# Squared norms and state reads as column-quarter products in a hybrid decoder step

## The chip, the cores and the metric

The kernel runs on one core of a Trainium2 chip. The time is device microseconds (us) of one execution. TensorE (PE) multiplies, VectorE (DVE), ScalarE (ACT) and GpSimd (POOL) do the element-wise work, SyncE (SP) issues most transfers. Each engine works through a queue of its own in the order fixed when the kernel is built; semaphores join the queues.

## The reference, cut to what matters

One inference step of a decoder layer for a prompt of 512 tokens and eight sample sequences with one token each. A projection feeds sparse attention (NSA) and a gated DeltaNet side by side; then come a merge, an output projection and an MLP. The change touches two places of the DeltaNet half.

```python
q, k, v = split(silu(conv(qkv)))          # 8 heads of 128 channels
q = _l2norm(q); k = _l2norm(k)            # x * rsqrt(sum(x*x over 128 channels) + EPS)
...
def step(state, xs):                      # for the sample: one token, state 128 x 128 per head and sequence
    v_new = u_c - w_c @ state             # reads the state by k
    o = q_c @ state + a_c @ v_new         # reads the state by q
    state = state * exp(gl_c) + k_c.T @ v_new
```

## The kernel before, in words

Channels lie on the 128 partitions, tokens along the free dimension: 512 of the prompt, then 8 of the samples. The fp32 inputs of the large products are split into two rounded parts, and `step` (L413) multiplies them in three products per slice of 128 channels (`bpg`, L153). These projections are cut into units of 128 output channels; they form one long stream. Everything else (recurrence, attention, the sample's work) is written as Python generators that `run` (L471) interleaves with the stream by an account of TensorE time, `pe_time`; each `yield n` asks for so much of the stream in between. A scheduler then orders the instructions of each engine at build time, by priority and by its own estimate of when operands are ready; so the order on an engine is not the order in the source.

**Quarters.** `quarters` (L163) makes four products that each write 32 partitions of one PSUM bank, partitions 32j to 32j+31, with a weight 32 columns wide. I call four of them with different j a *four*. They use different column quarters of the array. The first may be placed anywhere; the other three are only kept in order behind it, so other products may stand between them. Callers are the modulation projection (`ada`, L253: weight matrix `wa`, two fours in a row for each of 24 units), the sample's attention scores (`skT,Qz`, L1659, 8 fours) and its values (`arena` with `consts`, `pg` or `kvN`, L1697, 14 fours). All of these move 256 columns in fp32.

**Squared norms.** `norms` (L576) is called for each of 8 k heads (`ev_k`, L584) and 8 q heads (`ev_q`, L609), as soon as the projection of the head is evacuated, convolved and squared (tile `pre`). Four products with a column of ones, one for each 128 tokens, put the sum of the squares of a token into one PSUM column with tokens on partitions; DVE adds EPS, POOL raises it to -1/2, DVE makes two derived factors (`brk`, `brk2` or `rq`, `rq2`).

**State reads.** `dn_sample` (L1247) loads the sample's state in pieces of 128 x 4 x 128 (`Sx`, two for each of 8 heads). `read` (L1330) multiplies each of the 8 states of a head, as the weight, with the two columns `kq` (k and q of this sequence); six small DVE operations make `vn` of it. `vn` is turned (`consts,vn`), an outer product (`vbd,kst`) updates `Sx`, and SP writes it back (L1370) and loads the head after next (L1317).

**Buffers.** PSUM tags `ek` and `pg` have two banks each, `sp` (also called `sc`, `pt`) four. The SBUF tag `s2k` has four slots for `Sx`, pages and rows; `acc` (L1787), the sum of squares for the second norm, is a fifth user of it. `e2k` has four slots for evacuated rows.

fp32 products that are not transposes run as two instructions each in the trace; transposes and rounded products as one.

Of the kernel before, what the change touches and what calls it, by code (L numbers as in the profile page):

```python
# [7 lines left out]
F32 = mybir.dt.float32  # L8
# [3 lines left out]
ALU = mybir.AluOpType  # L12
# [5 lines left out]
T = S + NB  # L18
# [4 lines left out]
EPS = 1e-6  # L23
# [2 lines left out]
C_Q, C_KV, C_NG, C_DN, C_Z, C_A, C_B, C_M = 0, 1024, 2560, 2608, 5680, 6704, 6712, 6720  # L26
NRAW = 4
NKEEP = 8
CW = 3664
CR = 1024  # L30
SLOT = 528
ON_Q = "vector"
# [37 lines left out]
def hybrid_step(ctx: ExitStack, tc: tile.TileContext, A, O, dbg=None):  # L70


    nc = tc.nc
# [5 lines left out]
    wk = ctx.enter_context(tc.tile_pool(name="wk", bufs=10))  # L79
# [27 lines left out]
    def e2(name, dt=F32):  # L107
        return wk.tile([128, SLOT], dt, name=name, tag="e2k", bufs=4)
# [8 lines left out]
    def cst(shape, dt):  # L117

        n = 1
        for v in shape[1:]:  # L120
            n *= v
        r = dt == F32R
        x = (rounded if r else consts)[0:shape[0], cused[r]:cused[r] + n]
        cused[r] += -(-n // 8) * 8
        assert cused[r] <= (CW, CR)[r]
        x = x.bitcast(dt) if dt == I32 else x
        return x if len(shape) == 2 else x.rearrange("p (a b) -> p a b", a=shape[1])
# [12 lines left out]
    def bank(tag):  # L140
        tag = "sp" if tag in ("sc", "pt") else tag
        return ps.tile([128, 512], F32, name="b" + tag, tag=tag, bufs=4 if tag == "sp" else 2)
# [9 lines left out]
    def mm(out, lhs, rhs, start, stop):  # L152
        nc.tensor.matmul(out, lhs, rhs, start=start, stop=stop)  # L153
        n = 1
        for v in rhs.shape[1:]:
            n *= v
        pe_time[0] += n * (1 if rhs.dtype == F32R else 4) / 2400.0

    def tr(out, in_, idn):
        nc.tensor.transpose(out, in_, idn)  # L160
        pe_time[0] += 0.107

    def quarters(out, lhs, rhs, start, stop, n=1, order=(3, 2, 1, 0)):  # L163

        first = True
        for s in range(n):
            for j in order:
                r = nc.tensor.matmul(out[32 * j:32 * j + 32], lhs(j, s), rhs(j, s), start=start and s == 0, stop=stop and s == n - 1)
                if not first:
                    tc.keep_in_program_order(r)  # L170
                first = False
        pe_time[0] += 0.25 * n * rhs(0, 0).shape[-1] / 128
# [5 lines left out]
    for hf in range(2):  # L178
        c = slice(hf * 512, hf * 512 + 512)
# [11 lines left out]
    for t in range(5):  # L191
        src, n = x_rows(t)
# [18 lines left out]
    ident = cst([128, 128], F32)  # L211
    nc.vector.tensor_scalar(ident, jp, 0.0, None, op0=ALU.is_equal)
    ones = cst([128, 128], F32)
    nc.vector.memset(ones, 1.0)
    mhalf = cst([128, 8], F32)
    nc.vector.memset(mhalf, -0.5)
    cT = cst([128, 96], F32)
    nc.vector.memset(cT, 0.0)
    sel = cst([128, 9], F32)
    nc.vector.tensor_tensor(sel, ident[:, 0:9], ident[:, 32:41], op=ALU.add)  # L220
    for j in (64, 96):
# [334 lines left out]
    rq, rq2, brk = (smp[:, 96 + i * 32:128 + i * 32].rearrange("p (h c) -> p h c", c=4) for i in range(3))  # L556
    nsb, lns, brk2 = (smp[:, 192 + i * 32:224 + i * 32].rearrange("p (c h) -> p c h", h=DH) for i in range(3))
    slot = {}
# [14 lines left out]
        return out, e  # L573


    def norms(out, sq, eps):  # L576

        p = bank("ek")
        for t in range(4):
            mm(p[:, t:t + 1], sq[:, t * 128:(t + 1) * 128], ones[:, 0:1], start=True, stop=True)  # L580
        nc.vector.tensor_scalar(out, p[:, 0:4], eps, None, op0=ALU.add)
        nc.gpsimd.tensor_tensor(out, out, mhalf[:, 0:4], op=ALU.pow)

    def ev_k(i, P):  # L584
        y, e = yield from conv(8 + i, P, slot["kT"][:, i])
        nc.scalar.activation(e, slot["kT"][:, i], AF.Square)
        yield
        yield
        r = lns[:, :, i]
        norms(r, e, EPS)  # L590
        nc.vector.tensor_tensor(brk[:, i], r, slot["beta"][:, :, i], op=ALU.mult)
        nc.vector.tensor_tensor(brk2[:, :, i], r, brk[:, i], op=ALU.mult)

    tma, o_dn = Whole(), Whole()

    def bv(h, c):
        return o_dn[:, h, c * 128:(c + 1) * 128]
# [11 lines left out]
    def ev_q(i, P):  # L609
        y, e = yield from conv(i, P, slot["qT"][:, i])  # L610
        nc.scalar.activation(e, y, AF.Square)
        yield
        yield
        r = rq2[:, i]
        norms(r, e, EPS)
        nc.vector.tensor_scalar(rq[:, i], r, float(128 ** -0.5), None, op0=ALU.mult)
        nc.vector.tensor_tensor(r, rq[:, i], rq[:, i], op=ALU.mult)

    V = []

# [108 lines left out]
    for x in FILL.split():  # L729
        if x in nxt:  # L730
            n = nxt[x]
# [19 lines left out]
    for j in range(8):  # L751
        if j < 5:
            norm1(j)
        i = j // 2 + 4 * (j % 2)
# [447 lines left out]

    def nsa_tiles():

        masks = wk.tile([128, SLOT], F32, name="masks", tag="masks", bufs=1)
        mk = slot["mk"] = masks[:, 0:512]
        jp = token_gap()
        mc = slot["mc"] = cst([128, 4, 32], F32)
        with tc.issue_after(slot["late_v"].ins):
            nc.vector.memset(mk[:, 0:384], 0.0)  # L1210
            nc.vector.tensor_scalar(mk[:, 384:512], jp, 0.0, BM, op0=ALU.is_gt, op1=ALU.mult)
            for i in range(4):
                nc.vector.tensor_scalar(mc[:, i], cio, float(128 * i), BM, op0=ALU.is_gt, op1=ALU.mult)
        Kt = b16("K", F32R)
        Ks = slot["Ks"] = Kt[:, 0:2176].rearrange("p (g c) -> p g c", g=4)
        slot["Kw"] = Kt[:, 2176:4224].rearrange("p (g c) -> p g c", g=4)
        for g in range(NG):
            hi, lo = group_rows(g)
            with tc.issue_after(slot["late_a"].ins):
                nc.scalar.copy(out=Ks[hi, g, 0:32], in_=kcd[hi, g])  # L1220
            nc.vector.tensor_tensor(Ks[lo, g, 0:32], kcd[hi, g], f32(Ks[hi, g, 0:32]), op=ALU.subtract)
# [25 lines left out]
    def dn_sample():  # L1247
        dsc = kb4(q4, (1024,), F32, "dsc", "q4")
        r_k, r_q, qks, egs, bts, os_ = (dsc[:, i * 64:i * 64 + 64] for i in range(6))
        sy = dsc[:, 448:640].rearrange("p (m n) -> p m n", n=NB)  # L1250
        sq3 = dsc[:, 640:832].rearrange("p (a u) -> p a u", a=3)
        kq = dsc[:, 832:960].rearrange("p (u a) -> p u a", a=2)
# [15 lines left out]
        for hf in range(2):  # L1268
            p = bank("sc")
# [23 lines left out]
        p = bank("sc")  # L1293
# [18 lines left out]
        Sx = {}  # L1312
# [8 lines left out]
        for hf in range(2):  # L1321
            p = bank("sc")
# [7 lines left out]
        def read(h):  # L1330

            us = slice(h * 8, h * 8 + 8)
            p = bank("sc")
            for hf in range(2):
                for n in range(4):
                    u = h * 8 + hf * 4 + n
                    mm(p[:, (hf * 4 + n) * 2:(hf * 4 + n) * 2 + 2], Sx[h][hf][:, n], kq[:, u], start=True, stop=True)
            ks = p[:, 0:16].rearrange("p (n a) -> p a n", a=2)
            vn = wk.tile([128, 3, 8], F32, name="vn", tag="vn", bufs=4)
            nc.vector.tensor_tensor(vn[:, 0], ks[:, 0], egs[:, us], op=ALU.mult)  # L1340
            nc.vector.tensor_tensor(vn[:, 1], ks[:, 1], egs[:, us], op=ALU.mult)
            nc.vector.tensor_tensor(vn[:, 0], v_s[:, us], vn[:, 0], op=ALU.subtract)
            nc.vector.tensor_tensor(vn[:, 0], vn[:, 0], bts[:, us], op=ALU.mult)
            nc.vector.tensor_tensor(vn[:, 2], vn[:, 0], qks[:, us], op=ALU.mult)
            nc.vector.tensor_tensor(os_[:, us], vn[:, 1], vn[:, 2], op=ALU.add)
            return vn
        vn = read(0)
        for h in range(8):
            yield 4
            pv = bank("pt")  # L1350
            tr(pv[0:8, 0:128], vn[:, 0], ident)
            if h < 7:
                vn = read(h + 1)
            vr = vst[h % 2]
            vs = f32(vr)
            nc.scalar.copy(out=vr[0:8], in_=pv[0:8, 0:128])
            nc.vector.tensor_copy(vr[64:72], vs[0:8])
            nc.vector.tensor_tensor(vr[32:40], pv[0:8, 0:128], vs[0:8], op=ALU.subtract)
            r = [v4(e2("vbd", F32R)[0:72, 0:512]) for _ in range(2)]
            for hf in range(2):  # L1360
                nc.vector.tensor_tensor(r[hf], vs[:, None, :].to_broadcast([72, 4, 128]),
                                        m72[:, hf * 4:hf * 4 + 4, None].to_broadcast([72, 4, 128]), op=ALU.mult)
            yield 4
            for hf in range(2):
                p = bank("pt")
                mm(p, kst[h // 4][:, h % 4], r[hf].rearrange("p n v -> p (n v)"), start=True, stop=True)
                for n in range(4):
                    u = h * 8 + hf * 4 + n
                    nc.vector.scalar_tensor_tensor(Sx[h][hf][:, n], Sx[h][hf][:, n], egs[:, u:u + 1], v4(p)[:, n], op0=ALU.mult, op1=ALU.add)
                nc.sync.dma_start(sdo[:, hf * 4:hf * 4 + 4, h], Sx[h][hf])  # L1370
            if h < 6:
                s_load(h + 2)
# [411 lines left out]
                nc.vector.tensor_tensor(xi[:, S:T], xi[:, S:T], e, op=ALU.add)  # L1784
        return halves(P, f, hv)

    acc = wk.tile([128, SLOT], F32, name="acc", tag="s2k", bufs=4)[:, 0:T]  # L1787

    def ev_out(hf):
        c = half(hf)  # L1790

# [174 lines left out]
```

## Time and profile before

| | us |
|---|---|
| median of 3 runs | 1334.24 |
| lowest, highest | 1331.4, 1338.27 |
| profiled execution, its own time | 1336.41 |
| span of that execution | 1334.6 |

The profile comes from one execution. Its span is the time from the first to the last instruction; 1.8 us lie around it. In a row of products, the start times tell how long one holds TensorE: products are pipelined, so that each row's duration is longer than the distance to the next start. The granted TensorE clock was 0.962 of full speed on the mean.

| engine | busy us | share |
|---|---|---|
| PE | 1262.5 | 95% |
| DVE | 849.2 | 64% |
| ACT | 645.9 | 48% |
| POOL | 253.5 | 19% |

### The profile page before, as it was taken

The numbers are of one execution on the slowest core, as the hardware profiler recorded it, in microseconds if no ns is written. First come the engines' busy times: TensorE is split into PE (matmuls) and PEld (weight loads), VectorE is DVE, ScalarE is ACT, GpSimd is POOL, SyncE is SP. The second block draws the span as 40 slices with busy tenths as digits, with TensorE's granted clock in tenths as the row PEclk, the third lists the DMA queues.
The fourth block names the chain that finished last, engine by engine and source line by source line (L and its number), as shares of the span: only waits on it lengthen the run. The fifth ranks groups of instructions, "written<-read, shape, count | busy, mean of one in ns | idle before, by whom it ended". The sixth has DMA issues, their size and how long they took to land. (4 is left out here: it accounts for less than half of the span.)

```text
span 1334.6 us, 26655 instructions
## 1 busy us (share of the span) xinstructions
PE 1262.5 (95%) x10336; PEld 1189.2 (89%) x10336; DVE 849.2 (64%) x2328; ACT 645.9 (48%) x1540; POOL 253.5 (19%) x338
## 2 busy tenths in 40 slices
PE   4999899999899999899999899999999999999997
PEld 3799899999689999787778798889999999999997
DVE  2696958894345788876677777795853334334355
ACT  3484848653243335555555766684543142142233
POOL 2102100212111110312132233230242021021000
PEclk9799999998698999899999999999999999999999
DMA  8843311423333455335334211544642332424252
GB/s 250 255 135 107 101 49 49 117 83 94 119 111 92 116 142 156 106 97 155 93 114 140 82 55 33 143 129 110 163 112 75 97 94 81 110 80 117 74 158 96
DMA packets 235875, 149.82 MB, mean 112 GB/s; under 512 B 10331, under 2 KB 231059, under 8 KB 235485
## 3 DMA queue, kind: packets, MB, share of 16 engines
q1 hardware_dynamic: 226436, 135.84, 36.2%
q0 software_dynamic: 2240, 6.38, 1.6%
q10 hardware_dynamic: 7072, 5.90, 1.5%
q8 instruction: 81, 1.33, 0.4%
q14 instruction: 46, 0.37, 0.1%
HBM read 136.87 MB, written 15.60 MB: 114 GB/s over the span
## 5 line engine op out<-in xcount | busy, mean ns | idle before, releaser
L153 PE MATMUL bpg<-hh,wh 128*128 128x264 f32 (+1 forms) x1168 | 340.9, 292 | 6.8 <-ACT pre L493 1.4
L153 PE MATMUL bpg<-hh,wl 128*128 128x256 f32 (+1 forms) x1168 | 336.5, 289 | 2.1 <-DVE wl L398 2.1
L153 PE MATMUL bpg<-hl,wh 128*128 128x264 f32 (+1 forms) x1168 | 336.7, 288 | 0.0
L153 PEld LDWEIGHTS bpg<-hh,wh 128*128 128x128 f32 x1168 | 224.8, 193 | 9.6 <-issue 1.9
L398 DVE TENSOR_TENSOR wl<-raw,wh 128x1024 fp32r<-128x1024 f32 x149 | 182.7, 1228 | 69.7 <-ACT wh L394 51.6
L153 PEld LDWEIGHTS bpg<-hh,wl 128*128 128x128 f32 x1168 | 223.9, 192 | 3.6 <-DVE wl L398 3.0
L153 PEld LDWEIGHTS bpg<-hl,wh 128*128 128x128 f32 x1168 | 224.7, 192 | 1.6 <-issue 0.4
L394 ACT CAST wh<-raw 128x1024 fp32r<-128x1024 f32 x117 | 121.3, 1047 | 160.5 <-PE bpg L153 150.6
L153 PE MATMUL bpg<-act,wh 128*128 128x264 f32 (+1 forms) x1024 | 185.7, 283 | 0.0
L153 PEld LDWEIGHTS bpg<-act,wh 128*128 128x128 f32 x1024 | 157.4, 188 | 0.1
L153 PE MATMUL bpg<-act,wl 128*128 128x264 f32 (+1 forms) x512 | 144.7, 283 | 0.2 <-DVE wl L398 0.2
L153 PE MATMUL bpg<-h2h,wl 128*128 128x256 f32 (+1 forms) x448 | 126.8, 283 | 0.0
L153 PE MATMUL bpg<-h2h,wh 128*128 128x256 f32 (+1 forms) x448 | 126.5, 282 | 0.0
L153 PE MATMUL bpg<-h2l,wh 128*128 128x256 f32 (+1 forms) x448 | 126.2, 282 | 0.0
L1819 POOL TENSOR_TENSOR r<-r 128x520 f32<-128x520 f32 (+2 forms) x40 | 59.6, 1490 | 285.7 <-ACT r L1818 281.4
L1780 DVE SCALAR_TENSOR_TENSOR o_dn<-bpg,consts,o_dn 128x256 f32<-128x256 f32 x80 | 38.4, 483 | 98.3 <-PE bpg L153 98.2
L153 PEld LDWEIGHTS bpg<-act,wl 128*128 128x128 f32 x512 | 96.2, 188 | 0.5 <-DVE wl L398 0.4
L153 PEld LDWEIGHTS bpg<-h2l,wh 128*128 128x128 f32 x448 | 84.5, 189 | 0.0
L153 PEld LDWEIGHTS bpg<-h2h,wl 128*128 128x128 f32 x448 | 84.3, 188 | 0.0
L153 PEld LDWEIGHTS bpg<-h2h,wh 128*128 128x128 f32 x448 | 84.1, 188 | 0.0
L1446 POOL TENSOR_SCALAR consts<-consts,scl 128x32 f32<-128x32 f32 x64 | 25.7, 405 | 252.1 <-DVE scl L1441 87.6
L153 PE MATMUL bsp<-K,qst 128*128 128x288 f32 (+6 forms) x288 | 70.7, 320 | 2.2 <-DVE mx L1409 0.9
(625 smaller groups left out, 2571.1 us busy)
## 6 DMA issues: line engine op xcount, KB each, us to landing
raw<-in_w_in SPq DMA_DIRECT2D x68, 512.0 KB
wa<-in_w_ada SPq DMA_DIRECT2D x48, 512.0 KB
raw<-in_w_down SPq DMA_DIRECT2D x40, 512.0 KB
raw<-in_w_up SPq DMA_DIRECT2D x36, 512.0 KB
raw<-in_w_out SPq DMA_DIRECT2D x12, 512.0 KB
Sx<-in_state_dn SPq DMA_DIRECT2D x16, 256.0 KB
out_s_dn<-Sx SPq DMA_DIRECT2D x16, 256.0 KB
pg<-in_cache_k_slc SPq DMA_DIRECT2D x16, 128.0 KB
```

The costliest lines, as they stand in the source:

```text
L153: nc.tensor.matmul(out, lhs, rhs, start=start, stop=stop)
L394: nc.scalar.copy(out=wh, in_=raw)
L398: nc.vector.tensor_tensor(wl[:, 0:kp], raw[:, 0:kp], f32(wh[:, 0:kp]), op=ALU.subtract)
L1446: nc.gpsimd.tensor_scalar(x, x, sc[:, a_ * 3 + b_:a_ * 3 + b_ + 1], 1.0, op0=ALU.mult, op1=ALU.mult)
L1780: nc.vector.scalar_tensor_tensor(xi[:, q], p[:, 0:n], mod[:, m + i, 0:1], xi[:, q], op0=ALU.mult, op1=ALU.add)
L1819: nc.gpsimd.tensor_tensor(r, r, r, op=ALU.mult)
```

## The change

It does four things. (1) In `quarters`, the second to fourth product of each four (and all later rounds of the call) get a very high priority, so that the scheduler places them right behind the first. (2) `norms` now makes one four per head: the weight is a window of 32 columns of a constant that holds ones in one column only, the 512 squared tokens move past it as four times 128 columns, and the head's sums land in row h of each quarter. Four heads accumulate into one bank of `ek`, which they hold from the first head to the fourth. Then ACT copies the bank (`nrm`), one transpose turns it, and DVE and POOL work on 4 x 4 columns at once. (3) `read` takes the columns `kq` as the weight (32 of them, a pair of heads) and moves the state: two fours for a head, an ACT copy (`rd`), two transposes, then the same six DVE operations; there is a `yield 1.5` after the copy. (4) `acc` takes the tile of the attention masks in place of a slot of `s2k`. Constants grow by 72 columns.

```diff
@@ quarters
         for s in range(n):
             for j in order:
-                r = nc.tensor.matmul(out[32 * j:32 * j + 32], lhs(j, s), rhs(j, s), start=start and s == 0, stop=stop and s == n - 1)
+                with nullcontext() if first else tc.high_priority(20000):
+                    r = nc.tensor.matmul(out[32 * j:32 * j + 32], lhs(j, s), rhs(j, s), start=start and s == 0, stop=stop and s == n - 1)
@@ constants
+    one_of = cst([128, 64], F32)
+    nc.vector.memset(one_of, 0.0)
+    nc.vector.memset(one_of[:, 31:32], 1.0)
@@ norms
-    def norms(out, sq, eps):
-
+    norm_bank = {}
+
+    def norms(i, out, sq):
+
+        h = i % 4
+        if h == 0:
+            norm_bank[0] = bank("ek")
+        p = norm_bank[0]
+        quarters(p[:, 0:128], lambda j, s: one_of[:, 31 - h:63 - h], lambda j, s: sq[:, j * 128:j * 128 + 128], h == 0, h == 3)
+        if h < 3:
+            return
+        e = e2("nrm")[:, 0:128]
+        nc.scalar.copy(out=e, in_=p[:, 0:128])
+        yield
         p = bank("ek")
-        for t in range(4):
-            mm(p[:, t:t + 1], sq[:, t * 128:(t + 1) * 128], ones[:, 0:1], start=True, stop=True)
-        nc.vector.tensor_scalar(out, p[:, 0:4], eps, None, op0=ALU.add)
-        nc.gpsimd.tensor_tensor(out, out, mhalf[:, 0:4], op=ALU.pow)
+        tr(p[:, 0:128], e, ident)
+        t = wk.tile([128, 4, 4], F32, name="nsq", tag="nsq", bufs=2)
+        nc.vector.tensor_scalar(t, p[:, 0:128].rearrange("p (c h) -> p h c", c=4)[:, 0:4], EPS, None, op0=ALU.add)
+        nc.gpsimd.tensor_tensor(out, t, mhalf.rearrange("p (h c) -> p h c", h=4), op=ALU.pow)
@@ ev_k (ev_q likewise, with rq2 and rq)
-        r = lns[:, :, i]
-        norms(r, e, EPS)
-        nc.vector.tensor_tensor(brk[:, i], r, slot["beta"][:, :, i], op=ALU.mult)
-        nc.vector.tensor_tensor(brk2[:, :, i], r, brk[:, i], op=ALU.mult)
+        hs = slice(i - 3, i + 1)
+        r = lns[:, :, hs].rearrange("p c h -> p h c")
+        yield from norms(i, r, e)
+        if i % 4 == 3:
+            nc.vector.tensor_tensor(brk[:, hs], r, slot["beta"][:, :, hs].rearrange("p c h -> p h c"), op=ALU.mult)
+            nc.vector.tensor_tensor(brk2[:, :, hs].rearrange("p c h -> p h c"), r, brk[:, hs], op=ALU.mult)
@@ read
             p = bank("sc")
+            kq_ = kq[:, h // 2 * 16:h // 2 * 16 + 16].rearrange("p u a -> p (u a)")
             for hf in range(2):
-                for n in range(4):
-                    u = h * 8 + hf * 4 + n
-                    mm(p[:, (hf * 4 + n) * 2:(hf * 4 + n) * 2 + 2], Sx[h][hf][:, n], kq[:, u], start=True, stop=True)
-            ks = p[:, 0:16].rearrange("p (n a) -> p a n", a=2)
+                quarters(p[:, hf * 128:hf * 128 + 128], lambda j, s: kq_, lambda j, s: Sx[h][hf][:, j], True, True)
+            e = e2("rd")[:, 0:256]
+            nc.scalar.copy(out=e, in_=p[:, 0:256])
+            yield 1.5
+            p = bank("sc")
+            for hf in range(2):
+                tr(p[:, hf * 128:hf * 128 + 128], e[:, hf * 128:hf * 128 + 128], ident)
+            ks = [p[:, h % 2 * 16 + a:h % 2 * 16 + a + 239:34] for a in range(2)]
...
@@ nsa_tiles, and where acc stood
-        masks = wk.tile([128, SLOT], F32, name="masks", tag="masks", bufs=1)
+        masks = acc.t = wk.tile([128, SLOT], F32, name="masks", tag="masks", bufs=1)
...
-    acc = wk.tile([128, SLOT], F32, name="acc", tag="s2k", bufs=4)[:, 0:T]
```

What this makes of the order, at three places. On TensorE, in the sample's scores; `skT,Qz` are the quarters, `pg` transposes of cache pages, `bpg`, `K,qst` and `V` products of the stream and of the prompt's attention. Before:

```order
L153 MATMUL bpg<-hl,wh 128x256
L168 MATMUL bek<-skT,Qz 32x256
L153 MATMUL bek<-ptl,V_5904 128x256
L153 MATMUL bek<-pth,V_5904 128x256
L153 MATMUL bek<-ptl,V_5904 128x256
L160 MATMUL bsp<-consts,pg 128x128
L168 MATMUL bek<-skT,Qz 32x256
L160 MATMUL bsp<-consts,pg 128x128
L168 MATMUL bek<-skT,Qz 32x256
L160 MATMUL bsp<-consts,pg 128x128
L168 MATMUL bek<-skT,Qz 32x256
L160 MATMUL bsp<-consts,pg 128x128
```

The same four after:

```order
L153 MATMUL bpg<-hh,wl 128x264
L160 MATMUL bsp<-consts,ps 128x128 x2
L160 MATMUL bsp<-consts,pw 128x128
L169 MATMUL bek<-skT,Qz 32x256 x4
L160 MATMUL bsp<-consts,pw 128x128
L160 MATMUL bsp<-consts,pg 128x128 x8
```

One four stood in four separate places between other products, and now stands in one.

On TensorE at the norm of a q head, the fourth of its group after the change; `pre` is the tile of squares. Before:

```order
L153 MATMUL bpg<-hh,wh 128x264
L153 MATMUL bpg<-hl,wh 128x264
L153 MATMUL bpg<-hh,wl 128x264
L153 MATMUL bek<-consts,pre 128x1 x4
L153 MATMUL bpg<-hh,wh 128x264
```

After, with `nrm` the copy that ACT makes between the two steps:

```order
L153 MATMUL bpg<-hl,wh 128x264
L153 MATMUL bpg<-hh,wl 128x264
L169 MATMUL bek<-pre,consts 32x128 x4
L160 MATMUL bek<-consts,nrm 128x128
L153 MATMUL bpg<-hh,wh 128x256
```

Four products of one column became a four of 128 columns, and the transpose follows it with no product between.

On TensorE at the third state read; `consts,vn` turns the head before, `grhs` and `rt` are the recurrence. Before:

```order
L153 MATMUL bpg<-hh,wh 128x256
L153 MATMUL bsp<-grhs,rounded 128x512
L160 MATMUL bsp<-consts,vn 8x128
L153 MATMUL bsp<-dsc,Sx 128x2 x8
L153 MATMUL bsp<-grhs,rounded 128x512
```

After:

```order
L153 MATMUL bsp<-rt,LU 128x128 x4
L153 MATMUL bsp<-grhs,rounded 128x512
L160 MATMUL bsp<-consts,vn 8x128
L169 MATMUL bsp<-Sx,dsc 32x128 x8
L153 MATMUL bpg<-hh,wl 128x256
```

Eight products with two columns each became two fours; their two transposes (`consts,rd`) stand 26 rows further down.

## Rows read from the trace of the kernel before

**Rows 1.** Page, parts 1 and 2: busy time of engines; tenths and granted clock in 40 slices.
```profile
PE 1262.5 (95%) x10336; PEld 1189.2 (89%) x10336; DVE 849.2 (64%) x2328; ACT 645.9 (48%) x1540; POOL 253.5 (19%) x338
...
PE   4999899999899999899999899999999999999997
...
PEclk9799999998698999899999999999999999999999
```

**Rows 2.** What TensorE waited for: us in total, times, longest us.
```profile
PE bsp L160 <- DMA crow<-in_c_prompt: 15.6, 2, 13.5
PE bsp L160 <- POOL consts L1446: 9.2, 5, 4.0
PE bek L168 <- DMA wa<-in_w_ada: 7.8, 3, 4.1
...
PE bpg L153 <- DVE wl L398: 2.3, 4, 0.8
```

**Rows 3.** TensorE in order of time: start us, duration us; norm and read products.
```profile
299.76 0.95 PE L153 MATMUL bek<-consts,pre 128*128 128x1 f32 x8
...
493.35 1.05 PE L153 MATMUL bsp<-dsc,Sx 128*128 128x2 f32 x8
```

**Rows 4.** The same view: a four of the sample's scores in separate places.
```profile
606.09 0.28 PE L153 MATMUL bpg<-hl,wh 128*128 128x256 f32 x1
606.30 0.62 PE L168 MATMUL bek<-skT,Qz 128*32 128x256 f32 x2
606.85 0.38 PE L153 MATMUL bek<-ptl,V 128*128 128x256 f32 x1
607.07 0.28 PE L153 MATMUL bek<-pth,V 128*128 128x256 f32 x1
...
607.50 0.62 PE L168 MATMUL bek<-skT,Qz 128*32 128x256 f32 x2
608.05 0.33 PE L160 MATMUL bsp<-consts,pg 128*128 128x128 f32 x1
608.31 0.62 PE L168 MATMUL bek<-skT,Qz 128*32 128x256 f32 x2
```

**Rows 5.** The same view: a whole four, then two fours in one place.
```profile
692.82 0.39 PE L153 MATMUL bek<-pth,V 128*128 128x256 f32 x1
693.13 0.64 PE L168 MATMUL bek<-pg,arena 128*32 128x256 f32 x8
693.70 0.33 PE L153 MATMUL bsp<-K,qst 128*128 128x128 f32 x1
693.87 0.34 PE L153 MATMUL bek<-rounded 128*128 128x256 f32 x1
```
```profile
355.03 0.47 PE L153 MATMUL bsp<-grhs,rounded 128*128 128x512 f32 x1
355.44 1.07 PE L168 MATMUL bek<-wa,consts 128*32 128x256 f32 x16
356.44 0.61 PE L153 MATMUL bek<-consts,ma 128*128 128x9 f32 x4
```

**Rows 6.** The same view: four transposes of 128 columns in a row.
```profile
428.04 0.60 PE L160 MATMUL bek<-consts,kvt 128*128 128x128 f32 x4
```

**Rows 7.** In order of time: a visit on TensorE, the ACT copy that follows it.
```profile
494.34 0.63 PE L168 MATMUL bek<-wa,consts 128*32 128x256 f32 x6
...
495.05 0.37 ACT L258 COPY ma<-bek 128x256 f32<-128x256 f32 x1 [1.57 <-PE bek L168]
```

**Rows 8.** Busy time by stretch: us, PE, PEld, DVE, ACT, POOL, then granted clock.
```profile
580.00:740.00 160.00, 154.46 (x1181) 124.95 (x1180) 111.71 (x372) 86.45 (x259) 38.24 (x75) 0.99 0.42 123
740.00:860.00 120.00, 110.59 (x862) 100.55 (x861) 93.79 (x333) 80.80 (x257) 37.74 (x72) 0.94 0.28 80
```

**Rows 9.** Groups of instructions by line: busy us, mean ns of one, idle before.
```profile
L582 POOL TENSOR_TENSOR consts<-consts 128x4 f32<-128x4 f32 x16 | 19.3, 1208 | 145.3 <-DVE consts L581 108.0 <-DVE pre L563 21.7 <-DVE X L892 9.3
L273 POOL TENSOR_TENSOR consts<-consts 128x1 f32<-128x1 f32 (+1 forms) x10 | 5.9, 596 | 62.1 <-DVE consts L272 59.5 <-DMA wa<-in_w_ada 2.6
L394 ACT CAST wh<-raw 128x1024 fp32r<-128x1024 f32 x117 | 121.3, 1047 | 160.5 <-PE bpg L153 150.6 <-issue 4.2 <-DMA raw<-in_w_down 1.9
```

**Rows 10.** What SP's queue waited for: us in total, times, longest us.
```profile
SPq L1370 <- DVE Sx L1369: 49.4, 11, 11.1
```

More of the change, by code (lines that the diff above doesn't have):

```diff
@@ L28 @@
 NKEEP = 8
-CW = 3664
+CW = 3736
 CR = 1024
@@ L214, in hybrid_step @@
     nc.vector.memset(ones, 1.0)
-    mhalf = cst([128, 8], F32)
+    mhalf = cst([128, 16], F32)
     nc.vector.memset(mhalf, -0.5)
@@ L588, in ev_k @@
         yield
-        r = lns[:, :, i]
-        norms(r, e, EPS)
-        nc.vector.tensor_tensor(brk[:, i], r, slot["beta"][:, :, i], op=ALU.mult)
-        nc.vector.tensor_tensor(brk2[:, :, i], r, brk[:, i], op=ALU.mult)
-    tma, o_dn = Whole(), Whole()
+        hs = slice(i - 3, i + 1)
[4 more added lines that the diff above has]
+            nc.vector.tensor_tensor(brk2[:, :, hs].rearrange("p c h -> p h c"), r, brk[:, hs], op=ALU.mult)
+    tma, o_dn, acc = Whole(), Whole(), Whole()
     def bv(h, c):
@@ L613, in ev_q @@
         yield
[L614 to L617, printed above, removed]
+        hs = slice(i - 3, i + 1)
+        r = rq2[:, hs]
+        yield from norms(i, r, e)
+        if i % 4 == 3:
+            nc.vector.tensor_scalar(rq[:, hs], r, float(128 ** -0.5), None, op0=ALU.mult)
+            nc.vector.tensor_tensor(r, rq[:, hs], rq[:, hs], op=ALU.mult)
     V = []
@@ L1333, in read @@
             p = bank("sc")
+            kq_ = kq[:, h // 2 * 16:h // 2 * 16 + 16].rearrange("p u a -> p (u a)")
             for hf in range(2):
-                for n in range(4):
-                    u = h * 8 + hf * 4 + n
-                    mm(p[:, (hf * 4 + n) * 2:(hf * 4 + n) * 2 + 2], Sx[h][hf][:, n], kq[:, u], start=True, stop=True)
-            ks = p[:, 0:16].rearrange("p (n a) -> p a n", a=2)
+                quarters(p[:, hf * 128:hf * 128 + 128], lambda j, s: kq_, lambda j, s: Sx[h][hf][:, j], True, True)
[6 more added lines that the diff above has]
+            ks = [p[:, h % 2 * 16 + a:h % 2 * 16 + a + 239:34] for a in range(2)]
             vn = wk.tile([128, 3, 8], F32, name="vn", tag="vn", bufs=4)
-            nc.vector.tensor_tensor(vn[:, 0], ks[:, 0], egs[:, us], op=ALU.mult)
-            nc.vector.tensor_tensor(vn[:, 1], ks[:, 1], egs[:, us], op=ALU.mult)
+            nc.vector.tensor_tensor(vn[:, 0], ks[0], egs[:, us], op=ALU.mult)
+            nc.vector.tensor_tensor(vn[:, 1], ks[1], egs[:, us], op=ALU.mult)
             nc.vector.tensor_tensor(vn[:, 0], v_s[:, us], vn[:, 0], op=ALU.subtract)
@@ L1346, in read @@
             return vn
-        vn = read(0)
+        vn = yield from read(0)
         for h in range(8):
@@ L1352, in dn_sample @@
             if h < 7:
-                vn = read(h + 1)
+                vn = yield from read(h + 1)
             vr = vst[h % 2]
```

## The prediction

> **What bounds the kernel now.** I read the shares of the page first, then the waits of TensorE, then its order of time at the places that the change touches. TensorE is busy 95% of the span, and no other engine exceeds 64% [rows 1]; the slices stand at 8 or 9 tenths nearly throughout. Its waits are short: 15.6 us at the start for the conditioning rows, 9.2 us for POOL in attention, 7.8 us for modulation weights, 2.3 us for split weights of the stream [rows 2]. Busy is not the same as needed, though: a product's duration covers its drain. So I count starts. In the order of time the distance from one start to the next is what a product holds of the engine, and this is the currency of the sum. As the stream's work is fixed and is there from beginning to end, each us of TensorE taken out should shorten the span, unless a wait takes its place.
>
> **Unbroken fours: the largest term.** A lone quarter between other products: the product before it starts at 606.09 and would be followed 0.12 later, at 606.21; the two products behind start at 606.85 and 607.07 in place of 606.21 and 606.33. So one visit to the quarters' shape costs 0.74 us; in the string that follows, 607.50 to 608.31 less one transpose of 0.11 gives 0.70 [rows 4, 6]. A whole four costs hardly more: 692.82 to 693.87, less two ordinary distances of 0.12 and 0.11, is 0.82 [rows 5]. Two fours in one place: from 355.27 (355.03 plus the 0.24 that its 512 columns take, twice the 256-column distance) to 356.44 is 1.17, so an added four costs about 0.40 [rows 5]. I take 0.74 for a visit and 0.40 for each further round within it.
>
> The order of the two kernels gives the visits, counted along TensorE's queue. Scores of the sample: 24 before, 11 after, at most one round each: 13 x 0.74 = 9.6 us saved. Values of the sample: 15 visits with 6 further rounds become 6 with 8: 9 x 0.74 - 2 x 0.40 = 5.9. Modulation: 28 with 26 become 22 with 27: 6 x 0.74 - 0.40 = 4.0. Sum 19.5 us. Some scores' fours still stand in two places; they are in the 11.
>
> **Norms.** Before: 16 heads, each 8 instructions at 0.10 to 0.11 (0.95 less the last one's 0.25, over 7; likewise 1.05) [rows 3]: 0.85, together 13.6 us. After: 16 fours in 15 visits, plus 4 transposes at 0.11 [rows 6]. No row shows a four of 128 columns. Above it costs what 256 columns cost, 0.74 (0.40 when added); below, what is left of a visit if streaming were free, 0.74 - 0.40 = 0.34. I take the middle, since half the columns stream: 0.54, and 0.20 when added. 15 x 0.54 + 0.20 + 0.44 = 8.7; saved 4.9, bounds 1.7 to 8.1.
>
> The transposes are a new wait. ACT starts its copy 0.08 after a visit has drained (494.97 to 495.05) and takes 0.37 [rows 7]; with some 0.1 back to TensorE that is 0.55. In two of the four groups the transpose follows the four at once, in one there are two products between, in one seven. I take 2 us; it is 1.1 if only the two bare ones wait, and 6.4 if all four copies stand behind a weight cast of 1.05 on ACT [rows 9]. While TensorE waits there, the whole stream behind it waits.
>
> POOL's power on 16 columns is not in the trace: 1 column takes 0.60, 4 take 1.21, so 0.20 more each gives 3.7; at the least it is 1.2 [rows 9]. Four of them replace 16 of the small ones (19.3 us), off TensorE's path. The second k group is the one that is waited for (by the factors of the triangular stage): TensorE's order has 73 rows between its transpose and the first product of that stage, over 8 us at 0.12 each, which covers 3.7 and two DVE steps. The bank of `ek` held for four heads costs nothing as ordered: inside the four holds the queue has no product of other work that writes `ek`. DVE loses some 30 small operations, which hides the larger ones left.
>
> **Reads.** Before: 8 heads of 16 instructions, 2 x 0.85 each [rows 3]: 13.6 us. After: 16 fours in 12 visits and 16 transposes: 12 x 0.54 + 4 x 0.20 + 1.8 = 9.1; saved 4.5, bounds 1.3 to 7.7 by the same two ends. The eight ACT copies lie beside TensorE: 9 to 48 rows stand between a read's last four and its transposes in all but the first head, where it is two rows. The sample's chain gets longer by copy and distance, but its result is needed only at the end of attention.
>
> The page "TensorEngine Tiling (Array Packing)" of the Trainium skill, section Instruction Overhead, speaks against these two terms: it gives about 60 cycles for a small product, and a product of one column the same as one of 60. At 2.4 GHz that would be 25 ns, an estimate from the page; the old products would then cost 6.4 us in all rather than 27.2, and both terms together would be a loss of 11 us. The trace differs: 100 to 110 ns from start to start, with the full-width weight loaded for each [rows 3]. The row decides.
>
> **Smaller edits.** The mask tile that `acc` takes is read last by the scores, which end ahead of the first output projection in TensorE's order: no wait. The freed `s2k` slot can only let state loads start earlier. Two memsets at the start lie under its 15.6 us of waiting [rows 2].
>
> **What cover goes.** In 580 to 740 us, where most of the broken fours lie, TensorE is idle 5.5 us of 160 (3.5%); in 740 to 860, with the same attention but no such fours, 9.4 of 120 (7.8%), DVE at 70 and 78% [rows 8]. Taking 15.5 us (9.6 + 5.9) out of the first stretch also removes time in which DVE, ACT and POOL caught up. If the remaining 145 us idle at the rate of the second stretch, that is 11.3, or 6 us more. Ends: nothing, and all 15.5. I take 6.
>
> **Sum.** 19.5 + 4.9 + 4.5 = 28.9; less 2 and 6 gives 21 us. The span of 1334.6 becomes 1313.6, the profiled execution's 1336.4 becomes 1315.4; the median lies 2.2 below that execution, so 1313.
>
> **Rivals.** (a) *Cover lost whole.* The sample's and the prompt's attention are paced by DVE, ACT and POOL once the drains are gone, and waits for POOL (9.2 us now) grow. For it: DVE rises to 111.7 of 145, 77%, what the second stretch has. Against it: 77% is no bound. Time: 28.9 - 2 - 15.5 = 11.4, so 1323. (b) *Evacuation sets the pace.* All 12 new copies are waited for in full, 12 x 0.55 = 6.6 us rather than 2: 1318. For it: two bare transposes; against it: the distance behind seven of the reads. The same page, section PSUM Bottleneck, says that tiling speeds up the products but not the evacuation; here the copies are what it means. (c) *Slower: SP's queue.* SP waits in order for each updated state before writing it back, up to 11.1 us now [rows 10], and the stream's weight loads stand behind. The copy and the 9 to 48 rows before the transposes (up to 6 us) lengthen that wait at each head. TensorE starves once a wait outlasts the weights ahead, about two units of 48 products, 11 us. If four us were lost at all eight heads, 32 us would eat the 21: 1345. Against it: the whole run shows 2.3 us of waiting for weights [rows 2]. (d) *Cheap fours, no lost cover.* 128 columns at 0.34 and no waits: 19.5 + 8.1 + 7.7 = 35.3, so 1299. That the change does not do what it says is excluded by the order, save for the fours in two places.
>
> **How the numbers follow.** Forecast 1313: 0.59. (a) 0.17, (b) 0.11, (c) 0.06, (d) 0.07. The range takes the forecast with either end of the four's price (6 us up or down) and reaches into (a), (b) and (d): 1300 to 1327, leaving out (c), the far part of (a) and of (d). About 0.5%, 6.7 us, is what a measurement can tell from no change: faster means below 1327.5. That holds for the forecast, (b), (d) and most of (a): 0.87; within 0.5% 0.07, slower 0.06.
>
> **What would show it.** In the profile of the changed kernel: the scores' fours as one row of eight instructions, 0.8 from the product before to the product behind; a four of 128 columns near 0.54; gaps before the `nrm` transposes near 0.5; TensorE's idle time around 570 to 720 below 8%; waits for split weights still near 2 us. It is wrong if fours of 128 columns cost as much as those of 256, if the idle share in attention goes above 12%, or if SP's waits for the state make the stream wait.

## The result, and the profile after

The changed kernel takes 1318.42 us (median of 4 runs, 1315.97 to 1319.74) against 1334.13 for the kernel before: a ratio of 0.9876, 95% interval 0.9856 to 0.9896. Measured once more, beside other kernels, it gave 1315.52 against 1333.36, 0.9883 (0.9861 to 0.9905). It is faster by 15.7 us; the forecast was 21, its range 1300 to 1327.

The page of the changed kernel, parts 1 and 2 (busy time of TensorE, then tenths and granted clock in 40 slices), answers to [rows 1]:

```profile
PE 1230.0 (93%) x10356; PEld 1161.2 (88%) x10356; DVE 845.6 (64%) x2294; ACT 647.7 (49%) x1552; POOL 237.9 (18%) x326
...
PE   4898899999989999899998899999999999999997
...
PEclk9899999999689999899999899999999999999999
```

TensorE is busy 32.5 us less, but the span fell by 18.8 only: it now stands idle for longer. What it waits for answers to [rows 2] (us in total, times, longest us):

```profile
PE bsp L160 <- DMA crow<-in_c_prompt: 15.2, 2, 13.0
PE bek L169 <- DMA wa<-in_w_ada: 9.6, 4, 4.1
...
PE bsp L160 <- POOL consts L1471: 3.5, 3, 2.2
...
PE bsp L160 <- DVE mx L1434: 2.6, 2, 1.8
PE bek L169 <- ACT pre L602: 2.6, 2, 1.9
PE bpg L153 <- DVE wl L402: 2.2, 5, 0.8
PE bek L169 <- ACT pre L629: 2.2, 1, 2.2
PE bsp L153 <- DVE X L912: 2.1, 1, 2.1
...
PE bsp L153 <- ACT X L911: 1.5, 1, 1.5
...
PE bek L160 <- ACT nrm L592: 1.2, 2, 0.8
```

The wait for POOL in attention is shorter (3.5 us, 9.2 before), that for split weights `wl` the same. The waits for the squares of a q head (`pre` L629) and for `nrm` are new. That for the squares of two k heads (`pre` L602) is not; the kernel before had it too:

```profile
PE bek L153 <- ACT pre L586: 3.4, 2, 2.8
```

The waits for `X` belong to the compression of the KV cache, which the diff does not touch: the first of its two strings of products stands behind 384 products of the stream, and stood behind 429. `mx` are the row extremes of the prompt's attention; more of them below, under the reads.

The new fours, in TensorE's order of time: a lone norm four with the stream around it, one that waits for its squares, two fours with the transpose of `nrm` behind, and a four of the sample's scores.

```profile
299.38 0.28 PE L153 MATMUL bpg<-hh,wh 128*128 128x264 f32 x1
299.59 0.43 PE L169 MATMUL bek<-pre,consts 128*32 128x128 f32 x8
299.94 0.39 PE L153 MATMUL bpg<-hl,wh 128*128 128x264 f32 x1
300.17 0.29 PE L153 MATMUL bpg<-hh,wl 128*128 128x264 f32 x1
```
```profile
293.45 0.43 PE L169 MATMUL bek<-pre,consts 128*32 128x128 f32 x8 [2.16 <-ACT pre L629]
```
```profile
188.45 0.65 PE L169 MATMUL bek<-pre,consts 128*32 128x128 f32 x16
189.48 0.33 PE L160 MATMUL bek<-consts,nrm 128*128 128x128 f32 x1 [0.39 <-ACT nrm L592]
```
```profile
636.92 0.28 PE L153 MATMUL bek<-ptl,V 128*128 128x256 f32 x1
637.13 0.64 PE L169 MATMUL bek<-skT,Qz 128*32 128x256 f32 x8
637.70 0.44 PE L160 MATMUL bsp<-consts,ps 128*128 128x128 f32 x2
637.98 0.38 PE L160 MATMUL bsp<-consts,pw 128*128 128x128 f32 x2
```

Each four is one row of eight. The norm four takes 0.79 from the product before to the second behind, less two ordinary distances of 0.12: 0.55. The scores' four takes 1.06 up to the third product behind, less 0.12 and twice 0.11: 0.72.

The stretches that answer to [rows 8] (us, PE, PEld, DVE, ACT, POOL, clock, DMA share, GB/s):

```profile
560.00:710.00 150.00, 141.53 (x1190) 122.45 (x1189) 115.85 (x398) 84.42 (x256) 32.55 (x71) 0.99 0.47 137
720.00:840.00 120.00, 111.93 (x885) 103.36 (x884) 94.04 (x337) 81.59 (x259) 36.01 (x73) 0.94 0.28 80
```

TensorE is idle for 5.6% of the first (3.5% before) and 6.7% of the second (7.8%).

### The profile page after: what moved, and what is told of

Its sections match the earlier page's. It is cut to its first block, busy times and chain, and to the rows that moved or that the text cites. A ratio compares the mean times of both kernels' runs of the same rounds, so it can differ in the third digit from the quotient of the medians.

```text
span 1315.8 us, 26700 instructions
## 1 busy us (share of the span) xinstructions
PE 1230.0 (93%) x10356; PEld 1161.2 (88%) x10356; DVE 845.6 (64%) x2294; ACT 647.7 (49%) x1552; POOL 237.9 (18%) x326
## 4 chain that ended last, share of the span: by engine, by line
PE 45%; DVE 7%; ACT 3%; DMA 2%; issue 2%; POOL 1%; POOLq 0%; SPq 0%; ACTq 0%; DVEq 0%
PE bpg L153 36%; PE bsp L160 3%; PE bek L153 3%; PE bsp L153 2%; PE bek L169 1%; DVE wl L402 1%; DVE ptl L1490 1%; DMA raw<-in_w_in 1%; DMA raw<-in_w_up 1%; ACT ps L1458 0%; DMA raw<-in_w_out 0%; DVE wh L400 0%; ACT pw L1458 0%; DVE hl L1516 0%; DVE ps L1434 0%
## 5 line engine op out<-in xcount | busy, mean ns | idle before, releaser
L153 PE MATMUL bpg<-hh,wh 128*128 128x256 f32 (+1 forms) x1168 | 342.3, 293 | 5.9 <-ACT LU L705 1.9
L153 PE MATMUL bpg<-hl,wh 128*128 128x256 f32 (+1 forms) x1168 | 337.7, 289 | 0.0
L1841 ACT ACTIVATE r<-bpg 128x256 f32<-128x256 f32 (+1 forms) x64 | 24.6, 386 | 137.1 <-PE bpg L153 137.1
L153 PE MATMUL bsp<-K,qst 128*128 128x256 f32 (+6 forms) x288 | 69.1, 319 | 5.8 <-DVE rounded L1481 2.0
```

What stands on the lines that cost most here:

```text
L1841: yield from halves(P, lambda c, p: nc.scalar.activation(r_[:, c], p, AF.Relu), hv)
```

## The experiments

**How they are read.** Two sums were made for every kernel. TensorE's *count* prices each product of its order by start-to-start distances: 0.11 for a transpose or a rounded product of 128 columns, 0.12 for 256, twice that for fp32 in two instructions, 0.08 and 0.21 for the small products of the triangular stage, a visit to fours 0.34 and 0.21 for each round of 128 columns in it (0.55 for a lone four of 128, as measured above). The *lag* of a product is its start in the profile less the count of all products ahead. Lag of the kernel minus lag of the kernel before, at the same place, is the new waiting up to there. A lower clock is in it too, so "waiting" here means idle time and slower products together. Times in the table are (ratio - 1) x 1333 us; waits are those of the profiled run. They need not add up to the measured time, which comes from several runs: the profiled execution of before (1336.4) lies 2 to 4 us above the medians of that kernel, so that the new waits may be that much too small in all.

**The theories.** A: the time falls by the count, and waits stay small. C: cover is lost in the sample's attention, as forecast, and only there. B: any change in the order of the work brings waits of its own, at places that the changed part has nothing to do with. N: the norms bring their own waits ahead of 320 us.

```text
kernel                    time (95%: +-)   count   new waits by stretch of before's time, us
                          us               us      0-51  -178  -307  -354  -506  -593  -698  -922   end
changed (first profile)   -16.5 (2.7)     -30.5    2.3   2.9   6.1  -2.2  -4.3   4.2   1.6   1.2   0.5
f1 changed, again         -15.6 (2.9)     -30.5    0.3   3.8   4.6  -2.0  -4.0   4.1   1.7   0.8   0.4
e1 fours unbroken          -8.7 (2.5)     -21.9    0.5  -0.3   0.0  -0.7   2.3   0.2   6.5  -1.7   3.8
e2 norms                   +6.3 (2.0)      -5.4    1.1   1.8   4.4   1.3  -0.3   1.2   0.1  -2.7   0.0
e3 reads                   -4.3 (2.3)     -14.1    2.0   1.3   0.0  -1.9  -3.1   5.5   1.7  -3.2   3.4
e4 norms and reads         +1.6 (2.1)     -19.6    0.7   2.5   4.4   2.2  -1.7   4.0   1.9   4.1  -0.4
f2 without norms          -10.9 (2.8)     -26.3    2.4  -1.4   0.0  -0.9   4.5   4.1   3.5   2.9   1.2
f3 late squares            +0.9 (2.1)     -31.3    0.7   3.9   2.2   4.1   4.4   4.1   4.2   6.4   0.4
f4 order only              +2.3 (2.5)      -0.7   -0.3   1.9   0.0  -1.5   1.1   6.3   0.0  -5.1   0.4
g1 scores broken          -12.1 (2.9)     -26.4    0.2   1.9   4.4  -2.4  -5.2   4.0   2.0   1.8  -0.2
g2 acc in state pool      -21.3 (3.5)     -30.5    0.1   2.1   4.5  -0.9  -2.6   4.4   1.6   0.5  -0.2
g3 norms charged as old    -2.1 (2.3)     -31.3    1.6   4.3   5.9  -1.1   3.0   4.0   2.6   5.3   1.4
g4 compress later         -14.7 (3.0)     -32.8    1.3   6.7   2.7  -2.4  -5.5   8.7   3.8   3.6  -0.1
```

The stretches are: start; compression and k heads; v and q heads; triangular stage; recurrence; last state reads and first scores; scores and values of the sample; the prompt's attention; the rest.

**The parts alone.** e1 is the kernel before with

```diff
@@ quarters
-                r = nc.tensor.matmul(out[32 * j:32 * j + 32], lhs(j, s), rhs(j, s), start=start and s == 0, stop=stop and s == n - 1)
+                with nullcontext() if first else tc.high_priority(20000):
+                    r = nc.tensor.matmul(out[32 * j:32 * j + 32], lhs(j, s), rhs(j, s), start=start and s == 0, stop=stop and s == n - 1)
```

> The kernel before with the raised priority inside a four alone: products 2 to 4 of each four stay together, norms and reads as they were. Visits to the quarters' shape: sample's scores 24 to 8, its values 15 to 10, modulation 28 to 21. TensorE's distances from start to start sum to 21.9 us less than before. Theory A (count): the whole of it is gained, about 1312. Theory C (cover lost in the sample's attention only): 6 us of it come back as waits at 520 to 620 us, about 1318. Theory B (any change in the order of the work brings about 10 us of new waits, also ahead of 320 us): about 1322.

1323.99 us, ratio 0.9935 (0.9916 to 0.9954). Up to 354 us its lag is that of the kernel before, within 0.7 us. Of the 21.9 us of visits removed, 6.5 come back between the scores and the last value. TensorE in 600 to 700 us, before and e1:

```profile
600.00:700.00 100.00, 97.65 (x708) 73.64 (x707) 67.55 (x218) 53.32 (x159) 23.98 (x45) 1.00 0.43 122
```
```profile
600.00:700.00 100.00, 95.56 (x812) 80.35 (x811) 70.77 (x229) 56.05 (x166) 26.53 (x51) 0.97 0.43 129
```

104 instructions more in the same 100 us, twice the idle time (4.4 for 2.35), and a granted clock that now falls to its low level for a while (0.97 on the mean). The sum is near what B gave. The place is the sample's attention, as C said, though at 600 to 700 us and not at 520 to 620. Another 3.8 us are lost behind 922 us, 2.3 in the recurrence: neither was expected by C.

e2 is the kernel before with the new `norms` and their factors, e3 the same with the new `read`, e4 has both and the moved `acc`. In all three the old fours are as before, and the new calls alone pass `whole=True`:

```diff
@@ quarters
-    def quarters(out, lhs, rhs, start, stop, n=1, order=(3, 2, 1, 0)):
+    def quarters(out, lhs, rhs, start, stop, n=1, order=(3, 2, 1, 0), whole=False):
...
+                with nullcontext() if first or not whole else tc.high_priority(20000):
```

> The kernel before with the summed norms alone (fours of 128 columns kept whole, the old fours as they were). TensorE's count falls by 5.4 us. Theory A: less 2 us for the wait on ACT's copies, about 1331. Theory C: the same, since attention is as before. Theory B: the norms' part brings its own waits ahead of 320 us, so that nothing or less than nothing is left: 1334 to 1340. A lone four of 128 columns 0.55 us.

1338.29 us, 1.0047 (1.0032 to 1.0062): slower, as B said; A and C are out for this part. The new waits lie where the norms are: 1.8 us beside the k heads, 4.4 beside the q heads, and they stay.

> The kernel before with the state reads on quarters alone (new fours whole, the old ones as they were). TensorE's count falls by 14.1 us, some 5 of it from the reads themselves and 9 from 13 fewer broken visits that the changed order happens to give. Theory A: about 1320. Theory C: 3 to 4 us lost in the sample's attention, about 1323. Theory B: about 1328.

1329.15 us, 0.9968 (0.9951 to 0.9985), nearest to B. Between 506 and 593 us 5.5 us are lost, about what the reads themselves save.

> The changed kernel with norms and reads as there, but the old fours (modulation, scores, values) without the raised priority. TensorE's count is 19.6 us below the kernel before. Theory A: about 1315. Theory C: most of the broken visits stay in attention, so little cover is lost there: about 1316. Theory B: about 1324, with 10 us of new waits as in the changed kernel, lying in the same places.

1332.94 us, 1.0012 (0.9996 to 1.0027): all of 19.6 us is gone, twice what B gave. Norms' and reads' waits stand side by side (4.4 and 4.0), and 4 us more are lost in the prompt's attention.

**The whole, and its order.** f1 is the changed kernel again. f2 is the changed kernel with the old norms; f3 has two more steps between square and four; f4 is the kernel before with another cost in the planner:

```diff
@@ f3: ev_k, and ev_q alike
         yield
         yield
+        yield
+        yield
         hs = slice(i - 3, i + 1)
@@ f4
-YS = 1.6
+YS = 1.62
```

> The changed kernel as it stands, once more, so that the three runs beside it have it on the same chip. About 1318, ratio 0.988. Its parts alone gave 0.9935 (fours unbroken), 1.0047 (norms) and 0.9968 (reads); their sum is -4.9 of 1000, the whole gives -12.4, so the parts do not add up.

1315.52 us, 0.9883. The parts alone, -8.7, +6.3 and -4.3, make -6.7; the whole gives -15.6.

> The changed kernel with the old norms (a head's four column sums of one column each), so unbroken fours and reads only. TensorE's count is 4.2 us above the changed kernel's and 26.3 below the kernel before. Theory A (count): 1322, slower than the changed kernel. Theory N (the norms bring some 11 us of waits ahead of 320 us, as they did alone): 1312, faster than the changed kernel, with the waits of the products of X and w near 108 us and of the q heads' fours near 293 us gone.

1321.89 us, 0.9918 (0.9898 to 0.9939): A has the number, and N the place. With the old norms the waits ahead of 320 us are gone. Busy time in 180 to 320 us, without and with (f2, then the changed kernel):

```profile
180.00:320.00 140.00, 140.00 (x1172) 139.15 (x1171) 110.29 (x278) 85.69 (x185) 20.65 (x25) 1.00 0.32 88
```
```profile
180.00:320.00 140.00, 135.47 (x1132) 130.95 (x1131) 106.16 (x252) 82.30 (x185) 19.27 (x18) 0.99 0.30 82
```

At 307 us f2's new waits are 0.9 us, f1's 8.7. But f2 loses 4.5 in the recurrence where f1 gains 4.0, and more in attention, so that the kernel with the norms is the faster one after all, by 6.4 us where their count is 4.2. That this is an effect of the norms and not of the order they come with is not shown; f3 and, further down, g3 speak against it.

> The changed kernel with two more steps between the squares on ACT and the four that sums them. Count 0.8 us below the changed kernel's. If the norms lose their gain by TensorE's own waits for the squares (2.2 us at a q head near 293 us and 1.9 at another) these go, and the time is about 1314. If what costs is the place that the new steps have in the order of all the work (theory B), waits come elsewhere and it stays within 4 us of 1318, on either side.

1333.9 us, 1.0007 (0.9991 to 1.0022). Neither reading held. The wait for the q heads' squares did go. TensorE's waits between 188 and 318 us, f1 and then f3:

```profile
PE bek L169 <- ACT pre L629: 2.1, 1, 2.1
PE bek L160 <- ACT nrm L592: 1.2, 2, 0.8
PE bpg L153 <- DVE consts L964: 0.9, 1, 0.9
```
```profile
PE bpg L153 <- DVE consts L968: 0.9, 1, 0.9
PE bek L160 <- ACT nrm L592: 0.4, 1, 0.4
```

So these 2.9 us were the new norms' own. But against f1 16.5 us were lost in all, far more than the 4 that B allowed. The triangular stage and the recurrence, 320 to 410 us, in before, f1 and f3:

```profile
320.00:410.00 90.00, 82.14 (x849) 73.26 (x848) 35.29 (x91) 26.10 (x56) 12.82 (x12) 0.73 0.29 89
```
```profile
320.00:410.00 90.00, 82.54 (x907) 74.83 (x906) 38.39 (x95) 29.49 (x63) 13.87 (x12) 0.81 0.30 89
```
```profile
320.00:410.00 90.00, 78.66 (x831) 70.44 (x830) 38.55 (x86) 30.35 (x64) 12.56 (x12) 0.73 0.31 91
```

and the waits from 360 to 515 us, f1 and f3:

```profile
PE bsp L153 <- DVE f__4452 L1206: 3.3, 1, 3.3
...
PE bsp L169 <- DMA Sx<-in_state_dn: 2.3, 1, 2.3
```
```profile
PE bsp L169 <- DMA Sx<-in_state_dn: 4.4, 1, 4.4
PE bsp L153 <- DVE dsc L1311: 3.7, 1, 3.7
PE bsp L153 <- DVE f__4452 L1210: 3.3, 1, 3.3
```

A mean of 0.81 between the levels 1.2 and 2.4 GHz is 34 us of 90 at the lower one; 0.73, in f3 and in the kernel before, is 49 us. f1 gets through 907 instructions there, f3 through 831.

> The kernel before with one of the planner's costs at 1.62 in place of 1.60: the same instructions in another order, and TensorE's count as before within 0.7 us. Theory A and C: as before, 1332, within 2 us. Theory B (the order by itself moves the time by its waits): off by 4 to 10 us, on either side; then single differences of a few us between these kernels say little of the part that was changed.

1336.49 us, 1.0017 (0.9999 to 1.0036): the same instructions in another order. By the interval it is within 0.4% of the kernel before, so A cannot be told from a small B here; but single stretches differ by +6.3 and -5.1 us.

**The last four** are the changed kernel with one line different each: scores' fours without the priority (g1), `acc` back in `s2k` (g2), the planner's account `pe_time` set back after each norm four to what the old norm booked, and after the transpose of `nrm` to what it was (g3), `yield 5` for `yield 3` ahead of the compression's products (g4).

```diff
@@ g1, the call for skT; elsewhere whole=True
-    gp == 0, gp == 1)
+    gp == 0, gp == 1, whole=False)
@@ g2
...
-        masks = acc.t = wk.tile([128, SLOT], F32, name="masks", tag="masks", bufs=1)
+        masks = wk.tile([128, SLOT], F32, name="masks", tag="masks", bufs=1)
...
+    acc = wk.tile([128, SLOT], F32, name="acc", tag="s2k", bufs=4)[:, 0:T]
@@ g3, around the four
+        was = pe_time[0]
...
+        pe_time[0] = was + 4 * 4 / 2400.0
@@ g3, around the transpose of nrm
+        was = pe_time[0]
...
+        pe_time[0] = was
@@ g4
         need("kv"[kv] + "_cmp")
-        yield 3
+        yield 5
```

> The changed kernel with the raised priority left off in the fours of the sample's scores: these stand in 16 places in place of 11, those of the values in 7 in place of 6, and TensorE's count is 4.1 us higher. Theory A: 1320. Theory C (in attention waits fill what the fours give up): the same as the changed kernel, 1316, within 2 us. Theory B: off by up to 10 us on either side, by waits at places that have no scores.

1322.34 us, 0.9909 (0.9887 to 0.9931), its runs spread over 10 us. The median is A's; the profiled run, 1315.8, is C's, with 3 us less waiting than f1. The interval overlaps that of f1: inconclusive.

> The changed kernel with the accumulator back in the slot among the sample's states: the same instructions, TensorE's count the same, in a slightly different order. If that edit costs and gains nothing, as forecast, 1316 within 2 us. Theory B: a few us off.

1314.6 us, 0.984 (0.9814 to 0.9866). The edit to `acc` gains nothing that can be seen; without it the kernel is perhaps 6 us faster, the best measured, but the intervals overlap, and its profiled span (1312.8 us) is f1's within 0.7 us.

> The changed kernel, with the planner told that a head's summed norm costs TensorE what the old one was booked at (0.007 us in place of 0.25). The same instructions; count 0.8 us lower. The waits ahead of 320 us stay, as the products of X and w keep their new place in the order. Theory A: 1315. Theory B: another order, so up to 10 us off, on either side.

1332.05 us, 0.9984 (0.9967 to 1.0002). This is B at its clearest: the instructions of the changed kernel, in an order that an account alone has moved, 13.5 us slower than f1. On the profiled executions it is 16.2, and nearly half of that is products that take longer at a lower clock: TensorE is busy 1236.7 us for f1's 1229.3, with the same instructions, and idle 93.0 for 84.2. It loses in the recurrence (3.0 for -4.0, with one wait of 4.1 us for the state's DMA) and in the prompt's attention (5.3 for 0.8).

> The changed kernel with two more steps between the compression's transposes and its products of X and w. Count 2.3 us lower; the first string of X and w keeps its place, the second one moves up by 3 us. Theory A: 1313, the fastest so far. Theory B: 1308 to 1326, by where the waits fall.

1319.53 us, 0.989 (0.9867 to 0.9912), within B's range and 6 above A. The count fell by 2.3 us, and the waits at 51 to 178 and 506 to 593 us grew by more.

## Why the prediction was right, and where it was not

The forecast was faster by 21 us with 8 us of waits against 28.9 removed. Measured: 30.5 removed by the count, and 9.6 to 12.2 us of new waits (f1 and the first profile). On the profiled executions the gain is 18.6 us, 1336.4 to 1317.8. The remaining 3 us are the median's: the text set it 2.2 us below the profiled execution, which held before, while the changed kernel's lies 0.6 above its own. So the sign and the size held. But that the waits came out near 8 in all is luck: the norms and the reads cost about 10 us more than the sum had for them, and two things made up for it, 4 us less lost cover and 6 us gained between 307 and 506 us, which no step foresaw.

**Unbroken fours, 19.5: removed as said, not gained as said.** The visits are gone, and whole fours cost 0.72 and 0.55. Alone (e1) they bring 8.7 us, and 6.5 of the loss lie in the scores and values.

**Cover, 6: right mechanism, right size in e1 (6.5), too much in the changed kernel (1.6 and 1.7).** By the rows that the forecast was made from, TensorE's idle time in this attention grew from 5.5 to 8.5 us, 3 where 6 were said, and its share stayed below the 8% that the text named. Where the loss of cover ends and that of the reads (below) begins is a choice: from 506 to 698 us both together are 5.8. g1, which should have separated the cover from the count, does not.

**The four of 128 columns, 0.54: right (0.55).** The guess that streaming costs in proportion held, and with it both products' terms.

**The norms' wait, 2: this step failed.** It counted the wait of the transposes for the copy only, and that was a little less than said (1.2 us). What it left out is that a q head's four now waits for the squares of its head at the place where the scheduler puts it, and that the first products of X and w of the compression come to stand further ahead. In 51 to 307 us the nine profiles with the new norms lose 6.1 to 10.2 us, the four changed kernels without them (e1, e3, f2, f4) between -1.4 and 1.9. Between 178 and 307 us alone it is 2.2 to 6.1 against 0.0; of f1's 4.6 there, 2.9 are waits for squares and copies that are gone in f3. Saving 5.4 us of TensorE, the norms by themselves are a loss (e2).

**The reads, 4.5 with nothing against it: also too good.** In 506 to 593 us all ten profiles with the new reads lose 4.0 to 8.7 us, e1 and e2 0.2 and 1.2. f4, which has the old reads, loses 6.3 there as well, but by other things: its clock falls to a mean of 0.90 (0.94 in the kernel before, and in f1), and its waits are the old ones. What the ten share is a wait for `mx`, the row extremes that DVE makes for the prompt's attention: between 505 and 615 us TensorE waits 2.6 to 3.3 us for them in each of the ten, and at most 0.3 in before, e1, e2 and f4. The last update of the state (`vbd,kst`) starts at 573.9 us in f1 and 560.5 in before, so that its chain on DVE now runs beside this attention. That the chain is what holds up `mx` is likely, not shown; the prediction's sentence that the longer chain of the sample costs nothing does not stand.

**What gave it back.** From 307 to 506 us the changed kernel waits 6.0 to 6.5 us less than before, which no step foresaw. It is the clock. The same stretch of the stream in before, then in f1:

```profile
308.00:506.00 198.00, 189.52 (x1753) 176.52 (x1752) 120.26 (x316) 67.29 (x145) 28.72 (x26) 0.87 0.40 112
```
```profile
310.00:496.00 186.00, 176.28 (x1755) 163.46 (x1755) 115.31 (x288) 67.69 (x147) 30.00 (x27) 0.91 0.40 113
```

Nearly the same number of instructions takes TensorE 13.2 us less of busy time, of which some 6 are the count's, though it is idle 1.2 us more. The means are some 51 us at the lower level in before and 34 in f1. A product of the stream with 264 columns holds TensorE 0.22 us at the lower level (before, at 347 us) and 0.12 at the upper, so 17 us less of it are worth some 8 us, an estimate. Between the same places g1 and g4 have 0.91 as well and wait 7.6 and 7.9 us less, e3 and g2 0.90 and 0.89 and wait 5.0 and 3.5 less; e1, e2 and e4 have 0.87, as before, and gain nothing. f2, f3 and g3 (0.88, 0.86, 0.89) gain nothing either: TensorE is idle there 3 to 8 us more than before, with a wait of 4.1 to 4.4 for a state that is still on its way. Why the clock rises earlier in some orders than in others was not found.

**Rivals.** (b) has the number, 1318, by the wrong cause: the norms' copies cost 1.2 us of waiting, and no wait for a copy of the reads shows in the profile; (b) had 6.6. (c) did not come: split weights are waited for as before; SP's waits for updated states went down, not up (24.2 us for 49.4), and its queue shows only as TensorE's waits for the state, 0.4 to 2.6 us in the changed kernel. (a) and (d) are out by their times. The page "TensorEngine Tiling (Array Packing)" of the Trainium skill, section Instruction Overhead, was rightly set aside: by its 25 ns (an estimate from it) the norms and reads would have raised what the products hold of TensorE, and for the norms it fell by 5.4 us, with 0.55 for each new four as measured (e2).

## What to carry to other kernels

Where a scheduler sets the order, a change to one part is a change to the order of all. Here the same instructions in another order differ by 13.5 us (g3 against f1), nearly as much as the whole change brings, so a single variant says little of a part worth 5 us; look at the stretch in which the part lies, in several variants, and at the granted clock there before looking for other causes. Count what a product waits for at its new place, its operands included, and not only the new chain behind it. Time taken out of an engine that is 95% busy is not time gained: of 22 to 33 us removed, between nothing and 21 were.

## What the runs showed of the hardware

A four of 128 fp32 columns costs 0.55 us and one of 256 columns 0.72, alone between other products. The power on 16 columns, not in the trace of before, takes POOL 3.1 us, where [rows 9] let 3.7 be expected (group of instructions: busy, mean ns of one, idle before):

```profile
L598 POOL TENSOR_TENSOR consts<-nsq,consts 128x16 f32<-128x16 f32 x4 | 12.5, 3121 | 91.4 <-DVE nsq L597 89.5 <-DVE consts L527 1.9
```

The granted clock was not expected to differ between orders of one program. Its mean was 0.966 to 0.969 in the five runs of f1, 0.955 to 0.963 in the twelve of g3 and 0.954 to 0.964 in the twelve of f3; the runs of one kernel, before, spread from 0.959 to 0.969.
